# S5 chunk matrices built on the chip instead of read back from DRAM, in a hybrid S5 and MoE layer

## The chip, the cores and the metric

One core of a Trainium2 chip runs one layer of a decoder in f32. The metric is the device time of one execution in microseconds (us). The engines are PE (TensorE, products and transposes), ACT (ScalarE), DVE (VectorE), POOL (GpSimd) and SP (SyncE, which only issues DMAs here).

## The reference

For 256 tokens of width 1024, a token mixer (S5, a diagonal complex state space model with 48 groups of 16 channels and 64 states) runs beside a four-head attention into 256 fixed memory rows. Both read one input projection, and their outputs are concatenated, projected and normed. A mixture of 32 experts, four for each token, follows, and a second norm. Cut to what matters here:

```
xin = x @ w_in                                  # 768 channels u for S5, 256 for the queries
bu  = einsum('gph,blgh->lbgp', B, u)            # complex
x_l = A * x_(l-1) + bu_l                        # scan over the tokens, by group and state
y   = re(einsum('ghp,lbgp->blgh', C, x)) + d_skip * u
y   = gelu(y);  y = y * sigmoid(y @ w_glu + b_glu)
h   = layer_norm(alpha * x + concat(y, xattn(queries, mem)) @ w_out)
out = layer_norm(alpha * h + moe(h))            # 32 experts, top 4, w_gu and w_down in f32
```

## The kernel before, in words

The scan is cut into 32 chunks of 8 steps. A chunk's outputs are the sum of two products: its own inputs by a matrix made of K[k] = C A**k B (k from 0 to 7, with the skip added at k = 0), and the state ahead of the chunk by C A**k. For each group the first matrix is block Toeplitz: for output step t and input row k (k = 7 - s for input step s) it is K[t + k - 7], and zero where that is negative.

K is made at L544 to L566. Products `kb` of `ca_pad` with the powers `m1p` go through `kr` (ACT copies) and transposes `kc` into `k_sb`, where POOL adds the skip `dsk`. Then it goes through DRAM: L584 writes zeros in front of K in `kd`, three stores at L589 write K behind them, and three loads at L596 read overlapping rows of 2048 words, so that the eight partition blocks of a tile `tj` hold K shifted by one step each. The products at L745 (`yb<-tj,u_sb`, 96 by count) use it; behind them on PE come the memory's share of the output projection (`yp<-wo,att`), the second group of `yb` products (`yb<-m,xs`), the gate (`zp`), the rest of the output projection, the router, and the experts.

Around this place, in program order: `m1_turned` (transposes and ACT copies), the power tables `m20` (DVE, with a sum on POOL), the memory's keys (`kps`), the chunk states (`sip`, `stp`), the scores of the attention (`sc`), `m21` and `m22`, the softmax (`mx` on DVE, `prob` on ACT), the scan of the states on DVE (`tw`, `gt`, then `xs`), the memory's values (`vmp`), `pTp` (transposes of `prob`) and `pv`. PE, ACT and DVE keep the program's order (`pin`). DMAs are issued on SP. A DMA takes one of eight semaphores in turn, so a ninth waits for the first to land.

Large tiles share a pool of 22 buffers of 128 x 2048 words (`NBIG`, `big_tile`). A load into one of them is issued when the buffer's last reader is done. The experts' weights, 12 tiles an expert (8 `gu` at L1081, 4 `dn` at L1088), go through the same pool, so their loads start when the tiles of the stages ahead are given up, and then follow PE's release of the experts' tiles before.

Of the kernel before, what the change touches and what calls it, by code (L numbers as in the profile page):

```python
# [9 lines left out]
F32 = mybir.dt.float32  # L10
# [6 lines left out]
P = 128  # L17
D = 1024          # model width
NT = 256          # tokens
KT = D // P       # k-tiles of the model width  # L20
MIX = 768         # S5 channels
NG, NS, NH = 48, 64, 16   # S5 groups, states of a group, channels of a group
Q, NC = 8, 32     # steps of a chunk, chunks (t = Q * c + s)
NE = 32           # experts
CAP = 64          # slots of an expert in one round
ALPHA = 2.0 ** 0.25
LN_EPS = 1e-5
MISS = 8192.0     # put between the ranks of an expert's tokens and of all others
# [8 lines left out]
RND = 12582912.0  # 1.5 * 2**23: adding it rounds to the nearest integer  # L37
# [3 lines left out]
def kernel(  # L41
# [55 lines left out]
    def pin(ins):  # L97
        """Keeps an engine's instructions in the order of this program."""
        key = (ins.ins.engine, id(nc.cur_bb.bb))
        if key in last_of:  # L100
            tc.add_manual_dep(
                ins.ins, last_of[key],
                mybir.DependencyInfo(mybir.DependencyClass.NoSync, mybir.DependencyReason.DATA), reason="order",
            )
        last_of[key] = ins.ins.name
        return ins

    class Ordered:
        """An engine whose instructions keep the order of this program."""
# [26 lines left out]
    # ------------------------------------------------------------------ constants; a warm tensor engine  # L136
# [5 lines left out]
    def busy(n):  # L142
        """Products nobody needs, that keep the tensor engine's clock up."""
        ps = bank("busy") if n else None
        for _ in range(n):
            mm(ps[:, 0:P], ones, ones, True, True)

    busy(9)
    sga, sgc = small("sga", (P, 1)), small("sgc", (P, 1))   # by the half of the partitions: - + and + -
# [4 lines left out]
    # ------------------------------------------------------------------ loads, in the order of need  # L154
# [23 lines left out]
    dsk = small("dsk", (NH, NG, NH))  # L178
    SP.dma_start(dsk.rearrange("p g h -> p (g h)"), d_skip.partition_broadcast(NH))
# [11 lines left out]

    tt(dsk, dsk, ident[0:NH, 0:NH].unsqueeze(1).to_broadcast([NH, NG, NH]), ALU.mult, G)   # D[g, h] (h' = h)

    # ------------------------------------------------------------------ S5: the parameters, [(twice, p), group]
# [8 lines left out]
    # B: ba = [re; im], bb = [im; re]; C: ca = [re; - im], cb = [im; - re]; all [(re | im, p), g, h]  # L203
# [19 lines left out]
    # ------------------------------------------------------------------ x transposed  # L223
# [20 lines left out]
    # ------------------------------------------------------------------ projections  # L244
    # u, channels on partitions, in order of (s, c) for t = 8 c + s; from there to u_sb[(k, h), g, c], k = 7 - s
# [38 lines left out]
    def dve_exp(o, in_, n):  # L284
        """o = exp(in_), by 2**k * e**r; in steps."""
# [15 lines left out]
    def together(*chains):  # L301
        """The steps of independent chains, in turns."""
        chains = list(chains)
        while chains:
            chains = [c for c in chains if next(c, chains) is not chains]
# [11 lines left out]
    # sin and cos of ang = k pi + r, |r| <= pi / 2  # L317
# [3 lines left out]
    def series(o, coef, last):  # L321
        """o = last * sum of coef[k] r2**k"""
# [5 lines left out]
    def angle():  # L328
# [15 lines left out]
        # (sgn has come in between)  # L344
# [4 lines left out]
    def sign():  # L349
        """(-1)**k"""  # L350
# [14 lines left out]
    # powers of A = mag (cs + i sn): apw[:, 0 | 1, k] = re | im of A**k  # L365
# [14 lines left out]
    # coef = (A - 1) / lam  # L380
# [15 lines left out]
    # tables [re; re] and [- im; im]  # L396
# [31 lines left out]
    # ------------------------------------------------------------------ S5: A**k B and C A**k, [(re | im, p), gl, k, h]  # L428
    ptmp = [big_tile(f"ptmp{k}") for k in range(2)]

    def power(name, j, k0, m):
        """A**k m for k0 <= k < k0 + 8 and the groups from 16 j on."""
# [27 lines left out]
    # ------------------------------------------------------------------ S5: W[c] = (cs + i sn)**(8 c), [(a, p), (j, l), c]  # L460
# [43 lines left out]
    # the damping of a chunk, zero where a new sequence starts  # L504
# [4 lines left out]
    # queries of the memory, transposed: [(2 heads, 64), pair, n]  # L509
# [27 lines left out]
    # ------------------------------------------------------------------ memory: keys, scores  # L537
# [4 lines left out]
    # response of a chunk's outputs to its own inputs, [(k, h'), g, h], with the skip at k = 0; in memory behind zeros,  # L542
    # from where a chunk's matrix is T[(k, h'), t, g, h] = K[t + k - 7]
    kt_ = big_tile("k_sb")  # L544
    k_sb, zt = kt_[:, 0:768].rearrange("p (g h) -> p g h", h=NH), kt_[0:48, 768:1024]
    G.memset(zt, 0.0)
    kr = big_tile("kr")[:, 0:1536].rearrange("p (b n) -> p b n", b=3)
    for b in range(3):
# [8 lines left out]
        S.copy(kr[:, b, :], ps)  # L557
    for b in range(3):
        ps = bank(f"kc{b}")
        for l in range(4):  # L560
            tr(ps[:, P * l : P * l + P], kr[:, b, P * l : P * l + P])
        S.copy(
            k_sb.rearrange("p (j l) h -> p l j h", j=4)[:, 4 * b : 4 * b + 4],
            ps.rearrange("p (l j h) -> p l j h", l=4, j=4)[:, :, :, 0:NH],
        )
    tt(k_sb[0:NH], k_sb[0:NH], dsk, ALU.add, G)  # L566
    dbg("@M1B", None)
    # A**k B transposed, in its place: [(k, h), gl, (re | im, p)]
# [12 lines left out]
    dbg("@KW", None)  # L581
    row = 15 * 256
    kd = dram.tile([48, row], F32, tag="kd", name="kd")
    SP.dma_start(kd[:, 0 : 7 * 256].rearrange("r (k n) -> r k n", k=7), zt.unsqueeze(1).to_broadcast([48, 7, 256]))  # L584
    dbg("@KD", None)
    tj = []
    for j in range(3):
        kj = kd[16 * j : 16 * j + 16, :]
        SP.dma_start(  # L589
            bass.AP(tensor=kj.tensor, offset=kj.offset + 7 * 256, ap=[[256, Q], [row, NH], [1, 256]]),  # L590
            k_sb[:, 16 * j : 16 * j + 16, :].rearrange("p g h -> p (g h)"),
        )
    for j in range(3):
        t = big_tile(f"tj{j}")
        kj = kd[16 * j : 16 * j + 16, :]
        SP.dma_start(t, bass.AP(tensor=kj.tensor, offset=kj.offset, ap=[[256, Q], [row, NH], [1, 2048]]))  # L596
        t = t.rearrange("p (t g h) -> p t g h", t=Q, g=16)
        tj += [t[:, :, g, :] for g in range(16)]

# [11 lines left out]
    # ------------------------------------------------------------------ S5: what each chunk adds to its end's state  # L611
# [14 lines left out]
    # re, im of [(a, p), (j, l), c], g = 12 j + 2 l + a  # L626
# [14 lines left out]
    for i in range(2):  # L641
# [8 lines left out]
        scores.append(sc)  # L650

# [29 lines left out]
    # ------------------------------------------------------------------ S5: states between chunks  # L681
# [6 lines left out]
    # conj(W) S, then the damped sum over the chunks before  # L688
# [34 lines left out]
    # states before each chunk: W times that, one chunk later; [(re | im, p), (r, a), c]  # L723
# [15 lines left out]
    # ------------------------------------------------------------------ S5: outputs, [(j, c), t, gl, h]; bank l % 3  # L739
# [5 lines left out]
    for gl in range(12):  # L745
        for j in range(4):
            mm(
                y_out(gl, j).rearrange("p (t h) -> p t h", h=NH), u_sb[:, 12 * j + gl, :], tj[12 * j + gl],
                gl % 4 == 0, False, True,
            )  # L750
# [34 lines left out]
    # channels on partitions: tiles 0-3 are channels 192 j + (0 .. 127), tiles 4, 5 pairs of the rest  # L785
# [24 lines left out]
    # the router's weights behind the norm's: (n g + b) W + rb = n (g W) + (b W + rb)  # L810
# [29 lines left out]
    # ------------------------------------------------------------------ output projection, first norm  # L840
# [9 lines left out]
    def norm_of_stats(n):  # L850
        """The mean and 1 / sqrt(var + eps), after norm_stats of both halves."""
# [8 lines left out]
    iota64 = keep_t("iota64", (P, CAP))                                # slot - MISS  # L860
# [5 lines left out]
    lower = keep_t("lower", (P, P))                                    # 1 where the row comes before the column  # L866
# [36 lines left out]
    # ------------------------------------------------------------------ router  # L903
# [35 lines left out]
    def chosen(i, lgp):  # L939
        """The mask of each token's four experts."""  # L940
# [10 lines left out]
    def ranks(i, ps):  # L951
        """Ranks among an expert's tokens, MISS below."""
        stt(rk[:, i, :], msk[:, i, :], -MISS, ps, ALU.mult, ALU.add)

    def up_bias(n, sel):
        """Both halves of the first product, [(half of the columns, slot), 512] each: the bias first."""
# [26 lines left out]
    # ------------------------------------------------------------------ experts  # L983
    def gather(n, rank, base, between=lambda: None):
        """The tokens of an expert's slots, transposed; rank is [P, 1] by token tile."""
# [19 lines left out]
    def gates_t(n, og, k):  # L1005
        """The gates of one or two experts' slots, slots on partitions."""
# [324 lines left out]
```

## Time and profile before

| what | value |
|---|---|
| median of 3 runs | 1120.77 us (1116.89 to 1122.39) |
| the profiled execution (its span) | 1121.0 us |
| PE busy | 1053.1 us (94%) |
| DVE, ACT, POOL busy | 286.4, 142.5, 53.9 us |
| DMA | 428.56 MB, mean 382 GB/s |
| chain that ended last | PE 55%, DMA 42% of the span |
| of it, DMA tj<-kd | 4% |

The busy time of PE counts products in flight, so 94% does not say that PE is the limit. The chain follows the last instruction back to what released it at each step; a DMA in it is a time in which an engine had nothing else to do but wait for that transfer.

### The profile page before, as it was taken

To read this page: it belongs to the slowest core of one execution; us is meant where nothing else is said; L and a number is where in the kernel's file an instruction comes from. 1 tells how busy PE (TensorE), PEld (TensorE's weight loads), DVE (VectorE), ACT (ScalarE), POOL (GpSimd) and SP (SyncE) were. 2 spreads that over 40 slices of the span, in tenths; PEclk is the share of its full clock that TensorE was granted. 3 is DMA by queue.
4 is the path that set the end of the run, shared out by engine and by line. 5 is a ranking of instruction groups with operands and counts; after the bars stand their busy time and mean duration, and the time that the engine had idled before them with its cause. 6 is when DMAs were issued, how large, how long until landed. Compare 5 with 4: busy or idle time off the path is not lost.

```text
span 1121.0 us, 13652 instructions
## 1 busy us (share of the span) xinstructions
PE 1053.1 (94%) x5721; PEld 486.0 (43%) x5721; DVE 286.4 (26%) x631; ACT 142.5 (13%) x270; POOL 53.9 (5%) x53
## 2 busy tenths in 40 slices
PE   9975999999999999999999898999899999999994
PEld 8863754444444444444434343423343343434331
DVE  7984142121212111212111212111121212121204
ACT  4441201000000101010100000000000000010002
POOL 1650030000000000000000000000000000000001
PEclk9986999999999999999999999999999999999998
DMA  8988989999999999999999999999999999999992
GB/s 236 230 172 166 378 356 392 415 415 416 415 415 417 415 417 416 417 416 416 416 416 415 417 415 416 417 416 416 402 416 417 416 416 416 415 416 416 415 404 78
DMA packets 90022, 428.56 MB, mean 382 GB/s; under 512 B 15918, under 2 KB 19474, under 8 KB 56804
## 3 DMA queue, kind: packets, MB, share of 16 engines
q1 hardware_dynamic: 89668, 427.11, 98.1%
q8 instruction: 47, 0.77, 0.3%
q10 hardware_dynamic: 288, 0.52, 0.1%
q14 instruction: 19, 0.16, 0.0%
HBM read 425.03 MB, written 2.57 MB: 381 GB/s over the span
## 4 chain that ended last, share of the span: by engine, by line
PE 55%; DMA 42%; DVE 1%; SPq 1%; issue 0%; ACT 0%; ACTq 0%; POOL 0%; DVEq 0%
PE gu_e L122 22%; DMA gu_e<-in_exp_w_gu_dram 22%; DMA dn_e<-in_exp_w_down_dram 15%; PE dn_e L122 13%; PE xgp_e L122 7%; PE cb_e L122 4%; DMA tj<-kd 4%; PE yp L122 2%; DMA win<-in_l_w_in_dram 1%; PE zp L122 1%; PE atp_e L125 1%; PE yb L122 1%; DMA mem_sb<-in_mem_dram 1%; PE qps L122 1%; PE kps L122 1%; SPq L168 0%
## 5 line engine op out<-in xcount | busy, mean ns | idle before, releaser
L122 PE MATMUL gu_e<-gu_e,xg_e 128*64 128x512 f32 x2048 | 457.2, 595 | 27.9 <-DMA gu_e<-in_exp_w_gu_dram 27.3
L122 PEld LDWEIGHTS gu_e<-gu_e,xg_e 128*64 128x64 f32 x2048 | 141.3, 137 | 337.6 <-issue 250.2
L122 PE MATMUL dn_e<-dn_e,xl_te 128*64 128x512 f32 x1024 | 226.8, 596 | 0.7 <-ACT xl_te L116 0.7
L122 PEld LDWEIGHTS dn_e<-dn_e,xl_te 128*64 128x64 f32 x1024 | 70.7, 137 | 154.0 <-issue 126.5
L1028 DVE TENSOR_SCALAR xl_e<-gu_e 128x512 f32<-128x512 f32 x32 | 22.1, 692 | 430.6 <-PE gu_e L122 430.6
L122 PEld LDWEIGHTS xgp_e<-oh_e,h_sb 128*128 128x128 f32 x1024 | 118.1, 192 | 7.3 <-issue 4.3
L122 PE MATMUL xgp_e<-oh_e,h_sb 128*128 128x64 f32 x1024 | 118.2, 274 | 0.0
L1056 DVE COPY y_e<-dn_e 64x512 f32<-64x512 f32 x32 | 21.9, 683 | 252.7 <-PE dn_e L122 252.7
L116 ACT ACTIVATE sg_e<-xl_e 128x512 f32<-128x512 f32 x32 | 20.2, 630 | 404.3 <-DVE xl_e L1028 404.3
L122 PE MATMUL cb_e<-y_e,ogT_e 128*128 128x512 f32 x120 | 55.8, 604 | 0.0
L116 ACT COPY y_e<-dn_e 64x512 f32<-64x512 f32 x32 | 18.6, 581 | 257.6 <-DVE y_e L1056 250.4
L116 ACT COPY xg_e<-xgp_e 128x512 f32<-128x512 f32 x32 | 18.7, 585 | 155.3 <-PE xgp_e L122 155.3
L128 DVE TENSOR_TENSOR acc<-acc,cb_e 128x512 f32<-128x512 f32 x56 | 36.2, 683 | 6.6 <-PE cb_e L122 6.6
L122 PEld LDWEIGHTS cb_e<-y_e,ogT_e 128*128 128x128 f32 x120 | 21.7, 190 | 32.5 <-issue 29.7
L122 PE MATMUL gu_e<-bgu,ident 32*64 32x512 f32 x256 | 34.8, 612 | 0.0
L131 DVE TENSOR_SCALAR oh_e<-iota,rk 128x64 f32<-128x64 f32 x62 | 13.0, 252 | 66.7 <-PE xgp_e L122 66.7
L1125 POOL MEMSET bd<- 128x1280 f32 x1 | 1.2, 1164 | 583.4 <-PE gu_e L122 583.4
L1030 DVE TENSOR_SCALAR xr_e<-gu_e 128x512 f32<-128x512 f32 x32 | 22.1, 692 | 3.1 <-PE gu_e L122 0.2
L1031 DVE SCALAR_TENSOR_TENSOR xr_e<-xr_e,xl_e 128x512 f32<-128x512 f32 x32 | 22.0, 689 | 0.5
L1032 DVE TENSOR_TENSOR xr_e<-xr_e,sg_e 128x512 f32<-128x512 f32 x32 | 22.0, 687 | 0.6 <-DVE og_e L131 0.2
L122 PE MATMUL ups<-xT,win 128*128 128x256 f32 x96 | 21.5, 382 | 0.4 <-DMA win<-in_l_w_in_dram 0.4
L122 PE MATMUL yp<-wo,ymT 128*128 128x512 f32 x48 | 20.9, 595 | 0.0
(283 smaller groups left out, 580.4 us busy)
## 6 DMA issues: line engine op xcount, KB each, us to landing
gu_e<-in_exp_w_gu_dram SPq DMA_DIRECT2D x256, 1024.0 KB, 19.9
dn_e<-in_exp_w_down_dram SPq DMA_DIRECT2D x127, 1024.0 KB, 20.1
win<-in_l_w_in_dram SPq DMA_DIRECT2D x8, 512.0 KB, 10.2
wo<-in_w_out_dram SPq DMA_DIRECT2D x3, 1024.0 KB, 41.8
tj<-kd SPq DMA_DIRECT2D x3, 1024.0 KB
wgl<-in_l_s_w_glu_dram SPq DMA_DIRECT2D x2, 768.0 KB, 9.9
x_sb<-in_x_dram SPq DMA_DIRECT2D x2, 512.0 KB, 3.6
mem_sb<-in_mem_dram SPq DMA_DIRECT2D x1, 1024.0 KB
```

What stands on the lines that cost most here:

```text
L116: return f if name == "dma_start" else lambda *a, **k: pin(f(*a, **k))
L122: pin(PE.matmul(o, lhsT, rhs, start=start, stop=stop, skip_group_check=shared))
L125: pin(PE.transpose(o, in_, ident if idn is None else idn))
L128: return (eng or V).tensor_tensor(out=o, in0=x0, in1=x1, op=op)
L131: return (eng or V).tensor_scalar(out=o, in0=x0, scalar1=s1, scalar2=s2, op0=op0, op1=op1)
L1028: V.tensor_scalar(out=xl_, in0=ps[0], scalar1=7.0, scalar2=None, op0=ALU.min)
L1030: V.tensor_scalar(out=xr, in0=ps[1], scalar1=7.0, scalar2=-7.0, op0=ALU.min, op1=ALU.max)
L1031: V.scalar_tensor_tensor(out=xr, in0=xr, scalar=1.0, in1=xl_, op0=ALU.add, op1=ALU.mult)
L1032: V.tensor_tensor(out=xr, in0=xr, in1=sg, op=ALU.mult)
L1056: eng(y[:, 512 * dh : 512 * dh + 512], ps[dh][64 * dh : 64 * dh + 64, :])
L1125: G.memset(t[:, 0:width], 0.0)
```

## The change

K no longer goes through DRAM. `k_sb`, `kd` and the seven DMAs around it are gone. `kr` has 144 columns a group, 16 of zeros in front of 128, and the skip is added there, on all partitions. Three tiles `tz` are allocated and filled with zeros by POOL at the place where `k_sb` was. Behind the scores, each of the three gets two sets of four transposes out of `kr` (the second set from 16 columns earlier, which shifts by one step), each evicted by ACT into one step t of `tz`; then five ACT copies move pairs of steps to other partition blocks, 32 partitions further for two steps. `yb` reads its matrices from `tz`. For the skip on all partitions `d_skip` is loaded by four DMAs instead of one, and a DVE reduction makes the mask `same`. (Comments are taken out as well; those lines are not shown.)

```diff
-    dsk = small("dsk", (NH, NG, NH))
-    SP.dma_start(dsk.rearrange("p g h -> p (g h)"), d_skip.partition_broadcast(NH))
+    dsk = small("dsk", (P, 12, NH))
+    for j in range(4):
+        SP.dma_start(
+            dsk[32 * j : 32 * j + 32].rearrange("p g h -> p (g h)"),
+            d_skip[192 * j : 192 * j + 192].partition_broadcast(32),
+        )
...
-    tt(dsk, dsk, ident[0:NH, 0:NH].unsqueeze(1).to_broadcast([NH, NG, NH]), ALU.mult, G)
+    same = small("same", (P, NH))
+    V.tensor_reduce(
+        out=same, in_=ident.rearrange("p (j r) -> p r j", j=4)[:, 0:NH, :], axis=AX.X, op=ALU.add
+    )
+    tt(dsk, dsk, same.unsqueeze(1).to_broadcast([P, 12, NH]), ALU.mult, G)
...
-    kt_ = big_tile("k_sb")
-    k_sb, zt = kt_[:, 0:768].rearrange("p (g h) -> p g h", h=NH), kt_[0:48, 768:1024]
-    G.memset(zt, 0.0)
-    kr = big_tile("kr")[:, 0:1536].rearrange("p (b n) -> p b n", b=3)
+    kr_t = big_tile("kr")
+    kr = kr_t[:, 0 : 12 * 144].rearrange("p (b n) -> p b n", b=12)
+    G.memset(kr[:, :, 0:NH], 0.0)
+    tz = []
+    for b in range(3):
+        tz.append(big_tile(f"tz{b}"))
+        G.memset(tz[b], 0.0)
...
-        S.copy(kr[:, b, :], ps)
-    for b in range(3):
-        ps = bank(f"kc{b}")
-        for l in range(4):
-            tr(ps[:, P * l : P * l + P], kr[:, b, P * l : P * l + P])
-        S.copy(
-            k_sb.rearrange("p (j l) h -> p l j h", j=4)[:, 4 * b : 4 * b + 4],
-            ps.rearrange("p (l j h) -> p l j h", l=4, j=4)[:, :, :, 0:NH],
-        )
-    tt(k_sb[0:NH], k_sb[0:NH], dsk, ALU.add, G)
+        S.copy(kr[:, 4 * b : 4 * b + 4, NH:144], ps.rearrange("p (l n) -> p l n", l=4))
+    tt(kr[:, :, NH : 2 * NH], kr[:, :, NH : 2 * NH], dsk, ALU.add, G)
...
-    dbg("@KW", None)
-    row = 15 * 256
-    kd = dram.tile([48, row], F32, tag="kd", name="kd")
-    SP.dma_start(kd[:, 0 : 7 * 256].rearrange("r (k n) -> r k n", k=7), zt.unsqueeze(1).to_broadcast([48, 7, 256]))
-    dbg("@KD", None)
-    tj = []
-    for j in range(3):
-        kj = kd[16 * j : 16 * j + 16, :]
-        SP.dma_start(
-            bass.AP(tensor=kj.tensor, offset=kj.offset + 7 * 256, ap=[[256, Q], [row, NH], [1, 256]]),
-            k_sb[:, 16 * j : 16 * j + 16, :].rearrange("p g h -> p (g h)"),
-        )
-    for j in range(3):
-        t = big_tile(f"tj{j}")
-        kj = kd[16 * j : 16 * j + 16, :]
-        SP.dma_start(t, bass.AP(tensor=kj.tensor, offset=kj.offset, ap=[[256, Q], [row, NH], [1, 2048]]))
-        t = t.rearrange("p (t g h) -> p t g h", t=Q, g=16)
-        tj += [t[:, :, g, :] for g in range(16)]
...
+    tv = [t.rearrange("p (g t h) -> p g t h", t=Q, h=NH) for t in tz]
+    for b in range(3):
+        for a in range(2):
+            ps = bank(f"kc{b}{a}")
+            for l in range(4):
+                tr(ps[:, P * l : P * l + P], kr[:, 4 * b + l, NH - NH * a : NH - NH * a + P])
+            S.copy(tv[b][:, :, Q - 1 - a, :], ps.rearrange("p (g h) -> p g h", h=2 * NH)[:, :, 0:NH])
+        for m, rows in ((1, ((32, 64), (64, 96), (96, 128))), (2, ((64, 128),)), (3, ((96, 128),))):
+            for r0, r1 in rows:
+                S.copy(
+                    tv[b][r0:r1, :, Q - 2 - 2 * m : Q - 2 * m, :],
+                    tv[b][r0 - 32 * m : r1 - 32 * m, :, Q - 2 : Q, :],
+                )
+    tj = [tz[(g % 12) // 4][:, P * (4 * (g % 4) + g // 12) :][:, 0:P] for g in range(NG)]
```

## Rows read from the trace of the kernel before

**Rows 1.** The page, rate of DMA in 40 slices of 28 us.
```profile
GB/s 236 230 172 166 378 356 392 415 415 416 415 415 417 415 417 416 417 416 416 416 416 415 417 415 416 417 416 416 402 416 417 416 416 416 415 416 416 415 404 78
```
**Rows 2.** A window: us, busy by engine, PEclk, DMA share, GB/s.
```profile
190.00:560.00 370.00, 370.00 (x1942) 157.39 (x1943) 70.23 (x146) 33.96 (x62) 0.00 (x0) 1.00 1.02 416
```
**Rows 3.** Waits of the load queue, 172 to 200 us: total, times, longest.
```profile
SPq L1088 <- PE gu_e L122: 9.6, 3, 7.1
```
**Rows 4.** The chain in order of time: start us, us, what.
```profile
62.63 39.72 DMA tj<-kd
...
121.61 15.89 PE zp L122 x96
...
172.51 13.96 PE gu_e L122 x64
```
**Rows 5.** Timeline of PE: start us, us, what, [idle before <- releaser].
```profile
49.61 1.53 PE L125 MATMUL kc<-ident,kr 128*128 128x128 f32 x12
...
64.34 2.00 PE L122 MATMUL sc<-att 64*128 64x256 f32 x16
...
80.61 4.22 PE L125 MATMUL pTp<-ident,prob 128*128 128x128 f32 x16 [7.17 <-ACT prob L116]
...
88.03 0.41 PE L122 MATMUL yb<-tj,u_sb 128*32 128x128 f32 x4
...
102.39 5.27 PE L122 MATMUL yb<-tj,u_sb 128*32 128x128 f32 x90 [11.48 <-DMA tj<-kd]
107.59 7.13 PE L122 MATMUL yp<-wo,att 128*128 128x512 f32 x16
114.66 2.83 PE L122 MATMUL yb<-m,xs 128*32 128x128 f32 x96
```
**Rows 6.** Windows of PE's work and pauses, columns as in rows 2.
```profile
76.00:87.00 11.00, 5.85 (x24) 4.17 (x26) 8.32 (x13) 9.40 (x30) 0.27 (x2) 0.53 1.05 152
87.00:90.00 3.00, 1.44 (x14) 0.56 (x10) 2.93 (x3) 1.83 (x2) 0.00 (x0) 1.00 0.87 98
90.00:107.00 17.00, 5.20 (x90) 4.41 (x91) 6.89 (x8) 0.04 (x1) 0.00 (x0) 0.51 0.77 152
```
**Rows 7.** Timeline of DVE, from several windows.
```profile
44.36 0.27 DVE L116 TENSOR_TENSOR s<-cv 128x24 f32<-128x24 f32 x2
...
55.10 2.15 DVE L116 TENSOR_TENSOR mv__473<-mv__473 128x24 f32<-128x24 f32 x3
...
72.64 3.66 DVE L116 TENSOR_SCALAR mx<-mx 128x4 f32<-128x4 f32 x1
...
95.22 1.89 DVE L116 TENSOR_TENSOR xs<-tw 64x744 f32<-64x744 f32 x2
```
**Rows 8.** Groups by form, ACT, to 165 us: busy us, mean ns | idle before.
```profile
L116 ACT COPY ut<-ups 128x512 f32<-128x512 f32 x3 | 2.9, 1112 | 2.9 <-PE ups L122 2.9
...
L116 ACT COPY kr<-kb 128x512 f32<-128x512 f32 x3 | 1.8, 587 | 1.2 <-PE kb L122 1.2
...
L116 ACT COPY k_sb<-kc 128x256 f32<-128x256 f32 x3 | 1.1, 372 | 0.1
```
**Rows 9.** Timeline of ACT: the first exponential of the softmax.
```profile
76.41 0.47 ACT L116 ACTIVATE prob<-sc,mx 128x256 f32<-128x256 f32 x1 [11.32 <-DVE mx L116]
```
**Rows 10.** Timeline of SP: start us, us of issuing, what.
```profile
26.80 0.47 SPq L413 DMA_DIRECT2D mem_sb<-in_mem_dram  x1
...
108.42 15.09 SPq L1081 DMA_DIRECT2D gu_e<-in_exp_w_gu_dram  x8
```
**Rows 11.** Groups by form, POOL: busy us, mean ns | idle before.
```profile
L1125 POOL MEMSET bd<- 128x1280 f32 x1 | 1.2, 1164 | 583.4 <-PE gu_e L122 583.4
```
**Rows 12.** Timeline of POOL: start us, us, what, [idle before <- releaser].
```profile
44.31 0.30 POOL L546 MEMSET k_sb<- 48x256 f32 x1
...
51.69 5.29 POOL L128 TENSOR_TENSOR k_sb<-k_sb,dsk 16x768 f32<-16x768 f32 x1 [7.08 <-DVE s L116]
...
67.14 9.01 POOL L128 TENSOR_TENSOR m<-m,ptmp 128x2048 f32<-128x2048 f32 x2 [0.35 <-POOL r L607]
```

More of the change, by code (lines that the diff above doesn't have):

```diff
@@ L747 @@
             mm(
-                y_out(gl, j).rearrange("p (t h) -> p t h", h=NH), u_sb[:, 12 * j + gl, :], tj[12 * j + gl],
+                y_out(gl, j).rearrange("p (t h) -> p t h", h=NH), u_sb[:, 12 * j + gl, :], tj[12 * j + gl].rearrange("p (t h) -> p t h", h=NH),
                 gl % 4 == 0, False, True,
```

## The prediction

> **What bounds the kernel now.** I read the page's rates by slice first, then the chain of waits, then windows around the two places that they point to, and last the timelines of the engines there. [rows 1] shows three parts: a start in which DMA moves 166 to 236 GB/s, a ramp of three slices at 356 to 392, and a long flat stretch near 416 GB/s. [rows 2] says what the flat stretch is: from 190 to 560 us the queues move 416 GB/s with no gap. It is the load of the experts' weights, and nothing in the change touches its rate. So the end can move only if this stretch begins earlier. What begins it stands in [rows 3]: between 172 and 200 us the load queue's issues wait for PE, for gu_e products that give a buffer back, so at that point all 22 big buffers are full and the transfers have caught up with PE. From there the rest of the kernel hangs on the time at which PE reaches the first expert's products, 172.51 us [rows 4]. A microsecond by which PE gets there earlier should be a microsecond off the end, one for one, as long as the loads can again fill the buffers by then.
>
> What holds PE up before that is one item: the chain waits 39.72 us, up to 102.39, for tj to land [rows 4], the loads that the change removes. Not all of the 39.72 us is lost. In [rows 5] PE has other work until 88.03; there the first yb products (a chunk's response to its own inputs) start, and after six of them PE sits idle for tj, 11.48 us on end. Behind the wait the granted clock is half (0.51 in [rows 6]), so that 90 products take 5.27 us where the 96 of the later yb group take 2.83 [rows 5]. From 76 to 107 us the queues move 98 to 152 GB/s [rows 6].
>
> **Removed.** The four stores to kd, the three loads tj, and the wait for them. If yb runs from 88.03 without a pause, at the full clock (1.00 from 87 to 90 us in [rows 6]), its 96 products take 2.83 us and end at 90.9. The yp products behind it need wo and att, which PE did not wait for before, and take 107.59 to 114.66 = 7.1 us. The second yb group (states, with xs) then starts at 97.9 instead of 114.66: **16.7 us earlier**. Its other input, xs, is ready at 95.22 + 1.89 = 97.1 [rows 7], so DVE is the next to be late, but by less. If the clock came back late, yb at half takes 5.27 x 96 / 90 = 5.6, 2.8 us more, and yp for as long again 1.4 more; 4.2 us is my bound. [rows 5, 6] have it at full again 5 to 6 us after PE takes up work (80.61 to 87, 102.39 to 107). I take the full clock, because pTp and pv fill the 7 us ahead of yb, as they do now.
>
> **Added to ACT, the price that counts.** 21 instructions go in front of the softmax: six evictions of 128x256, and fifteen copies of 512 elements a partition (32 or 64 partitions). An eviction of this size takes 372 ns, a 512-element copy 587 [rows 8]; the partitions do not enter. Sum 6 x 0.372 + 15 x 0.587 = 11.0 us. In the profile ACT idles 11.32 us just there, up to 76.41, where the softmax starts after mx [rows 9]. So the gap nearly holds the block. It can start when sc is done, 66.34, plus four transposes at the 1.53 / 12 = 0.13 us of kc's [rows 5], 0.5, less 0.1 for what moves ahead of it (below): 66.7. It ends at 77.8. The softmax starts **1.4 us later** than now, and pTp, pv, yb and xs with it (xs at 98.5). Bounds of a shifted copy: not under the 0.372 us of half its elements (then the block ends at 74.5, mx decides, and the softmax starts 1.2 us earlier than now), and up to 1.112 us, the price of ut [rows 8], whose writes are scattered word by word; then the block takes 18.9 us, and the softmax starts 9.2 us later. The copies here write runs of 32 words, nearer to kr's evictions than to ut's, so I take 0.587.
>
> **Moved and added on PE.** Twelve kc transposes leave the path at 50 us, 1.5 us [rows 5], and 24 come after sc, 3.1 us. These, and vmp behind them, which may also wait a few us for a PSUM bank that ACT gives back, lie in the idle stretch of 7.17 us before pTp [rows 5]; without that cover they would cost those 3.1 us.
>
> **Added at the start.** d_skip comes in four DMAs instead of one: three more issues on SP in front of mem_sb, whose own takes 0.47 us, at 26.80 [rows 10]. Memory keys and K then come up to 1.4 us later, against the 1.5 us that PE saves: net 0.1 earlier. One small reduction on DVE lies in the time before the first load lands. On SP nothing else moves; seven issues disappear, and the loads of wo, wgl and x that sat among them can only come earlier.
>
> **POOL.** Three fills of 128x2048 and a small one. At 1.16 us for 1280 columns [rows 11] a fill of 2048 is 1.8, so 5.4 us together. They would stand where the small k_sb fill stands now, 44.31, and be done near 50, before kr is there. The skip's addition shrinks from 16x768, 5.29 us, to 128x192, about 0.4 by m's 2048 in 4.5 [rows 12]. That matters to DVE: when the present addition got to run, DVE's three tiny mv_ products took 2.15 us in place of some 0.5 [rows 7]. So DVE gets about 1.2 us back, and with it POOL's m sums, which end at 67.14 + 9.01 = 76.15 [rows 12] and release mx (the 3.66 us row of [rows 7] ends just behind them). mx moves to 75.2 and stays in front of ACT's 77.8. For the fills the bounds are 0 and, if each held DVE as the additions do, 5.4 + 0.4 in place of 1.6: 4.2 us on DVE, the softmax at 80.6, 2.8 us behind my 77.8. I take 0: the k_sb fill ran from 44.31 to 44.61, and DVE's two s products of two SBUF inputs took 0.27 together beside it [rows 7, 12].
> [...]
>
> **Big buffers.** tz takes three of the 22 from about 44 us on, where tj took its three at 61, and kr stays until 67; k_sb's is gone. If that leaves one short, it is a load of wgl or wo that waits, and zp, the first to need wgl, starts at 121.61 now [rows 4] and about 106 then. The last of them can be issued when prob has been read, by 80.61 + 4.22 + 1.4 = 86.2 [rows 5], and has 20 us to spare, with no tj in its way.
>
> **Sum.** PE reaches the second yb group 16.7 - 1.4 = 15.3 us earlier, at 99.4, and from there on the work is what it was, so the first expert starts at 157.2. Do the weights follow? Their first tiles take buffers that come free at yb's end (about 92) and with xs (98.5); 20 tiles of 2.5 us (1.05 MB at 416 GB/s) are there near 149, before 157. So the shift reaches the end: 1121.0 - 15.3 = 1105.7. The profiled span is 0.2 us above the median of the runs, 1120.77; I say **1105.5 us**. The three runs lie 0.5% apart (1116.89 to 1122.39), so 0.5% is also about what this kernel's measurement tells from no change.
>
> **Rivals.**
> *The front eats half of it* (0.15). Fills that hold DVE (+2.8), a clock that comes back late (+4.2), or shifted copies at ut's price (9.2 in place of 1.4, +7.8): one alone gives 1108 to 1113, two together up to 1117.5. For it: the softmax has no slack, by [rows 7, 9] it starts with mx. Against: the rows by which each was taken at its low end.
> *The end does not move by PE's shift* (0.06). If the weights could not begin before 108.42, as now [rows 10], because wo, wgl and x stay slow without tj (152 GB/s in [rows 6]), 20 tiles would end at 158.4, and only what the queues lose later could be won: in the three slices of the ramp (378, 356, 392 against 416, 28 us each) some 8 us. With a delay of the front on top the time is 1113 to 1119. Against: in the first of these slices the queues, rid of tj, move 378 GB/s at once [rows 1].
> *Slower* (0.04): the shifted copies wait on one another, each for the writes of the one before, and ACT's block becomes the path. It breaks even where it lasts 11.0 + 15.3 = 26.3 us, at (26.3 - 2.2) / 15 = 1.61 us a copy; at 2.2, twice ut, it lasts 35.2, the softmax starts at 101.9 instead of 76.41, and the time is 1120.8 - 16.7 + 25.5 = 1129.6. Against: the rows nearest to these copies are all under 1.12 us.
> *yb still waits* (0.02), now for a tz that is late, because a fill stands behind a buffer still in use: between 1106 and 1121, by the hold.
>
> **Numbers.** The forecast has 0.73; its own range is 1100 (the softmax 1.2 us earlier instead of 1.4 later, 1102.9, less half the runs' spread) to 1109. With the front's rival the range is 1100 to 1114. Faster by over 0.5% (under 1115.2): 0.73 + 0.13 + 0.03 + 0.01 = 0.90. Within 0.5%: 0.06, the rest of the three mild rivals. Slower: 0.04.
>
> **What would show it.** In the profile after: yb in one piece of about 2.8 us near 89.4, with no DMA in front; the second yb group near 99.4; ACT busy without a gap from 66.7 to 77.8 with copies of 0.5 to 0.6 us, and softmax after it; POOL fills at 44 to 50 with DVE's tiny products beside them at their usual price; the first gu_e near 157; the flat 416 GB/s from about 175. I am wrong if the copies take over 1 us, if the fills stretch DVE's chain past 60 us, or if the weights' queue no longer waits on PE at the first expert, for then the end was not PE's to move.

## The result, and the profile after

The changed kernel takes 1108.56 us (median of 4 runs, 1108.34 to 1110.52) against 1120.9 of the kernel before on the same chip: ratio 0.9894, 95% interval 0.9876 to 0.9911, so 1.1% faster and clear of noise. The forecast was 1105.5, its range 1100 to 1114. The profiled execution has a span of 1108.8 us, 12.2 less than before; it is the longest of the four (1110.52 us), so its rows are those of one execution.

The rates of DMA by slice, as in [rows 1]:

```profile
GB/s 230 240 139 274 408 258 408 417 415 416 414 416 416 416 415 416 417 416 417 416 417 415 415 416 416 416 416 415 400 417 416 416 416 416 415 417 416 415 406 82
```

The flat stretch is what it was. The ramp is another: 408 GB/s from the fifth slice on (about 111 us), and then a dip to 258 that [rows 1] doesn't have. In the dip, from 139 to 149 us (107 GB/s), the queues have caught up with PE and wait for buffers.

PE's timeline, to be laid beside [rows 5]:

```profile
65.66 2.00 PE L122 MATMUL sc<-att 64*128 64x256 f32 x16
...
84.14 4.08 PE L125 MATMUL pTp<-ident,prob 128*128 128x128 f32 x16 [2.19 <-ACT prob L116]
88.91 3.68 PE L122 MATMUL pv<-pT,att 128*64 128x256 f32 x16 [0.69 <-ACT pT L116]
92.52 3.42 PE L122 MATMUL yb<-tz,u_sb 128*32 128x128 f32 x96
95.87 7.13 PE L122 MATMUL yp<-wo,att 128*128 128x512 f32 x16
102.94 2.83 PE L122 MATMUL yb<-m,xs 128*32 128x128 f32 x96
...
160.78 2.79 PE L122 MATMUL gu_e<-gu_e,xg_e 128*64 128x512 f32 x12 [0.68 <-ACT xg_e L116]
```

The first yb products run in one piece, with no DMA in front. The second group starts at 102.94 instead of 114.66, the first expert at 160.78 instead of 172.51: both 11.7 us earlier. The load queue still waits for PE at the first experts, as in [rows 3] (waits of SP, 160 to 190 us):

```profile
SPq L1088 <- PE gu_e L122: 10.8, 4, 7.1
```

ACT's block, in ACT's timeline, begins at 68.32 and ends where the softmax starts, 79.93, which was 76.41 in [rows 9]:

```profile
68.32 0.77 ACT L116 COPY tz<-kc 128x256 f32<-128x256 f32 x2 [1.92 <-issue]
69.12 3.13 ACT L116 COPY tz<-tz 32x512 f32<-32x512 f32 x5
...
79.93 0.47 ACT L116 ACTIVATE prob<-sc,mx 128x256 f32<-128x256 f32 x1
```

POOL's timeline (first fence) has the fills where they were expected, and DVE's (second fence) its tiny products beside them and the maximum of the softmax:

```profile
44.82 5.31 POOL L557 MEMSET tz<- 128x2048 f32 x3
53.07 2.92 POOL L128 TENSOR_TENSOR kr<-kr,dsk 128x192 f32<-128x192 f32 x1 [2.94 <-ACT kr L116]
```

```profile
45.05 0.49 DVE L116 TENSOR_TENSOR s<-e__485 128x24 f32<-128x24 f32 x4
...
55.41 1.05 DVE L116 TENSOR_TENSOR mv__478<-mv__478 128x24 f32<-128x24 f32 x3
56.38 2.28 DVE L116 TENSOR_TENSOR m<-cab,tab 128x2048 f32<-128x2048 f32 x1
...
71.27 3.56 DVE L116 TENSOR_SCALAR mx<-mx 128x4 f32<-128x4 f32 x1
```

Windows (columns as in [rows 2]) show the granted clock below full speed (means of 0.66, 0.57 and 0.51) in three short stretches. In the first of them PE had waited 2.28 us for mem_sb:

```profile
35.00:40.00 5.00, 4.46 (x21) 4.33 (x22) 5.00 (x4) 2.35 (x4) 5.00 (x4) 0.66 1.08 350
...
73.00:77.00 4.00, 4.00 (x14) 3.26 (x12) 3.19 (x4) 3.90 (x8) 1.81 (x1) 0.57 0.81 144
...
87.00:94.00 7.00, 6.31 (x53) 3.91 (x57) 6.86 (x7) 3.69 (x8) 0.00 (x0) 0.51 0.67 190
```

### The profile page after: what moved, and what is told of

The parts are those of the page before. It is cut to its first block, busy times and chain, and to the rows that moved or that the text cites. A ratio compares the mean times of both kernels' runs of the same rounds, so it can differ in the third digit from the quotient of the medians.

```text
span 1108.8 us, 13702 instructions
## 1 busy us (share of the span) xinstructions
PE 1056.9 (95%) x5733; PEld 487.9 (44%) x5733; DVE 285.5 (26%) x632; ACT 153.0 (14%) x288; POOL 55.6 (5%) x56
## 4 chain that ended last, share of the span: by engine, by line
PE 58%; DMA 37%; ACT 2%; DVE 1%; SPq 1%; issue 1%; ACTq 0%; POOL 0%; DVEq 0%
PE gu_e L122 24%; DMA gu_e<-in_exp_w_gu_dram 22%; PE dn_e L122 13%; DMA dn_e<-in_exp_w_down_dram 13%; PE xgp_e L122 7%; PE cb_e L122 4%; PE yp L122 3%; DMA win<-in_l_w_in_dram 1%; PE zp L122 1%; ACT tz L116 1%; PE atp_e L125 1%; DMA mem_sb<-in_mem_dram 1%; PE qps L122 1%; PE kps L122 1%; ACT prob L116 1%
```

## The experiments

Twelve kernels ran, each timed in five rounds against the kernel before. In those marked *, yb reads zeros, so each chunk's response to its own inputs is left out. "Left" is what the queues still had to move after 190 us, summed over the packets that end later; the rate beside it is that of a window. Times are in us.

| kernel | second yb | first expert | GB/s, 149 to 190 | left, MB | span | median | ratio |
|---|---|---|---|---|---|---|---|
| before | 114.66 | 172.51 | 359 | 377.19 | 1121.0 | 1120.9 | |
| after | 102.94 | 160.78 | 383 | 372.32 | 1108.8 | 1108.56 | 0.9894 |
| 1 round trip beside it, into DRAM | 101.71 | 159.55 | 386 | 371.68 | 1106.6 | 1108.35 | 0.9883 |
| 2 copies twice | 108.68 | 166.53 | 348 | 374.78 | 1114.4 | 1117.25 | 0.9962 |
| 3 skip's loads late | 98.56 | 156.41 | 381 | 370.50 | 1104.3 | 1106.68 | 0.9869 |
| 4 copies shared with DVE | 97.53 | 155.77 | 382 | 370.18 | 1103.1 | 1104.80 | 0.9847 |
| 5 both | 97.22 | 155.72 | 383 | 370.15 | 1103.9 | 1105.56 | 0.9859 |
| 6 before, yb without tj* | 107.59 | 165.38 | 415 | 374.64 | 1114.9 | 1116.09 | 0.9953 |
| 7 before, tj in 16-row loads | 99.58 | 157.43 | 406 | 370.96 | 1105.2 | 1107.05 | 0.9872 |
| 8 before, tj alone | 105.63 | 163.49 | 416 | 374.36 | 1114.4 | 1116.45 | 0.9947 |
| 9 before, yb without tj, tj held* | 97.44 | 159.24 | 417 | 374.18 | 1116.5 | 1119.78 | 0.9979 |
| 10 as 9, plain rows of weights* | 97.56 | 155.45 | 391 | 369.77 | 1102.3 | 1105.36 | 0.9858 |
| 11 as 9, the pattern on weights* | 97.27 | 159.12 | 417 | 374.35 | 1116.6 | 1116.64 | 0.9946 |
| 12 as 11, no overlap* | 97.21 | 155.11 | 417 | 372.53 | 1111.6 | 1114.17 | 0.9927 |

Two columns are to be read together. In every row the span is 190 us, plus what is left at 416 GB/s, plus 23 to 27 us. So the end goes with how much the queues have moved by then. The rate says what held them: at 348 to 391 GB/s they had gaps, waiting for PE to give buffers back; at 415 to 417 they had none, and were simply late (run 7 lies between). The expectations name their theories A and B anew in each run.

### 1. The round trip's traffic, put back beside the change

```diff
+    SP.dma_start(kd[:, 0 : 7 * 256]..., tz[0][0:48, 0:256]...)
+    for j in range(3):
+        SP.dma_start(<kd behind the zeros>, tz[j][:, 0:256])
+    for j in range(3):
+        td = dram.tile([P, 2048], F32, tag=f"td{j}", name=f"td{j}")
+        SP.dma_start(td, <the overlapping rows of kd>)
```

> The changed kernel with the transfers of the old round trip put back, with nothing waiting for them: the zero store, three stores to kd (of zeros), and three loads of 2048-word overlapping rows, which go to DRAM instead of SBUF, so another 3 MB is written. The results do not use them. Theory A (the end follows PE's arrival at the experts, and PE lost its wait for tj): no wait, no loss; 1108.6 us, at most 2 more from loads that come later. Theory B (the gain is the 3.8 MB and the slow queues that went): the gain is given back, 1118 to 1121.

1108.35 us (0.9868 to 0.9897): as fast as without the traffic. That spoke for PE's arrival alone, but too soon. These loads end in DRAM, and their 8 KB packets took 311 to 355 ns, where those of tj into SBUF took 737 to 957 (means over 5 us each) between 65 and 100 us in the kernel before. The bytes were put back, the slow transfer was not. Runs 9 to 12 make good for that.

### 2. Each shifted copy twice

```diff
-            for r0, r1 in rows:
+            for r0, r1 in rows + rows:
```

> The changed kernel with each of the fifteen shifted copies on ACT made twice, so ACT's block in front of the softmax is 15 x 0.626 = 9.4 us longer. A: every us of it goes to the end, 1118 us; second yb group 9.4 later than in the changed kernel. B: the end stays at 1108.6, give or take 1, for no transfer has changed.

1117.25 us (0.9950 to 0.9974). The softmax starts at 87.97, the second yb group 5.74 us later than in the changed kernel, and the span is 5.6 longer. By the medians the difference is 8.7 us, near the 9.4 of A. B is out: with free queues (348 GB/s, gaps) a delay of PE reaches the end, in the profiles one for one.

### 3. The skip's four loads later in the program

```diff
-    for j in range(4): SP.dma_start(dsk[...], d_skip[...])      # ahead of mem_sb
...
     SP.dma_start(wv, mem_w_v...)
+    for j in range(4): SP.dma_start(dsk[...], d_skip[...])
```

> The changed kernel with the four loads of d_skip issued behind wv instead of ahead of mem_sb, and POOL's product with the mask moved to its use. A, with the clock's drop at 35.8 us caused by the later mem_sb: mem_sb is issued near 26.2, the clock stays at full, PE has its 2.6 us back and the scores end near 65, ACT's block 2.6 earlier: 1106.0. If the delay of PE's front has another cause than these loads: 1108.6.

1106.68 us (0.9855 to 0.9884). sc starts at 63.56 instead of 65.66, the softmax at 77.84, and the granted clock from 35 to 40 us is 1.00 instead of 0.66. pv takes 2.00 us and yb 2.83, both at full clock. In the profiles the second yb group is 4.4 us earlier and the span 4.5 shorter.

The time is near A's 1106.0, but not for A's reason. On SP the four loads still went out ahead of the memory's, although they stand behind them in the program:

```profile
25.38 1.81 SPq L421 DMA_DIRECT2D dsk<-in_l_s_d_dram  x4
...
27.70 0.47 SPq L415 DMA_DIRECT2D mem_sb<-in_mem_dram  x1
```

mem_sb is issued at 27.70, as in the changed kernel (27.74), and not near 26.2. The earlier front did not come back in run 5, which has the same edit. By the medians the gain is 1.9 us, and the intervals of the two ratios overlap (0.9855 to 0.9884, 0.9876 to 0.9911). So no run shows a gain by this edit.

### 4. Ten of the fifteen copies on DVE

```diff
+        if b == 0:
+            shifts(b, S.copy)
...
         sums.append(sm)                  # behind the second mx
+    shifts(1, V.tensor_copy)
...
             S.mul(prob...)               # behind the reciprocals
+    shifts(2, V.tensor_copy)
```

> The changed kernel with ten of the fifteen shifted copies moved from ACT to DVE, five behind mx and five behind the reciprocals of the softmax, where DVE idles. A: the softmax starts with mx at 74.9 instead of 79.9, and the end comes 5 us earlier, 1103.6, less what xs gains of delay on DVE (its slack to PE is 2.3 us). B: 1108.6.

1104.80 us (0.9834 to 0.9860), clear of the changed kernel's interval and the lowest median of all, though not clear of runs 5 and 10. ACT's and PE's timelines show the next limits, mx and then xs:

```profile
75.09 0.47 ACT L116 ACTIVATE prob<-sc,mx 128x256 f32<-128x256 f32 x1 [1.10 <-DVE mx L116]
```

```profile
98.15 2.61 PE L122 MATMUL yb<-m,xs 128*32 128x128 f32 x88 [0.20 <-DVE xs L116]
```

### 5. Runs 3 and 4 together

> The changed kernel with both edits of before: ten shifted copies on DVE, and d_skip loaded behind wv. With the ten copies away the softmax waits for mx (POOL's m sums, done near 74.9), not for ACT's block; an earlier PE front then has no one to give its time to. A: the same as with the split alone, 1104.8, at most 1 less. If the two gains simply added up: 1104.8 - 1.9 = 1102.9.

1105.56 us (0.9844 to 0.9874): no more than run 4, as A said. The second yb group waits for xs, 1.13 and 0.44 us:

```profile
97.22 0.43 PE L122 MATMUL yb<-m,xs 128*32 128x128 f32 x8 [1.13 <-DVE xs L116]
```

So an earlier PE would have had nothing to gain here. It was not earlier, though: sc starts at 65.82, and mem_sb is issued at 28.37. Whether the gains of 3 and 4 are the same microseconds is therefore not shown.

### 6. The kernel before, with yb reading zeros

```diff
-                ..., u_sb[:, 12 * j + gl, :], tj[12 * j + gl],
+                ..., u_sb[:, 12 * j + gl, :], zer.rearrange("p (t h) -> p t h", h=NH),
```

> The kernel before with its whole round trip through DRAM, loads of tj into SBUF included, but the first yb products read a tile of zeros instead of tj: the chunks' own response and the skip are left out of the output, and nothing waits for tj. A: yb near 88, the second yb group near 98, zp perhaps held some 2 us for wgl, which lands near 107 while tj's transfers are under way: 1104 to 1108. B (the transfers themselves cost the time): 1119 to 1121.

1116.09 us (0.9939 to 0.9966), between the theories. ACT's timeline says why the front gained little: the tiles of tj that nobody read were given to the softmax as its output, which then waited for them.

```profile
86.12 0.47 ACT L116 ACTIVATE prob<-sc,mx 128x256 f32<-128x256 f32 x1 [21.20 <-DMA tj<-kd]
```

The wait had moved, so this run settles nothing by itself; run 9 is its repair.

### 7. tj in loads of 16 rows

```diff
-        SP.dma_start(t, <8 blocks of 16 rows of kd>)
+        for k in range(Q):
+            SP.dma_start(t[16 * k : 16 * k + 16], <16 rows of kd from block k>)
```

> The kernel before, round trip kept and used, with each of the three tj loads (outermost 8 blocks of 16 rows) cut into eight loads of 16 rows of 2048 words, the same bytes from the same places. If the slowness of these loads (3 MB in 40 us, packets of 8 KB at 0.72 to 0.96 us) comes from how one load of that shape is spread, they land before 88 and the wait is gone without any work for ACT: 1104 to 1107. If it comes from reading the same rows many times: no change, 1121, or slower by the 24 issues on SP at about 0.5 us each.

1107.05 us (0.9856 to 0.9888): the round trip is still there, and the kernel is as fast as the changed one. yb starts at 89.76 without a wait. A window while the loads run:

```profile
65.00:82.00 17.00, 9.92 (x56) 8.11 (x54) 14.52 (x11) 5.25 (x21) 13.00 (x5) 0.89 1.02 137
```

All 16 DMA engines are taken (share 1.02), yet they move only 137 GB/s. Two things had changed at once: the cut, and that tj was alone, since wo waited until 82.68 behind the 24 loads on SP.

### 8. tj alone, uncut

```diff
-    wo += load_wo(0)
+    wo0 = big_tile("wo0")...
...
             S.mul(prob...)
+    S.copy(wo0[0:1, 0, 0:1], prob[0:1, 1, 3, 0:1])
+    SP.dma_start(wo0, ov[0:P, 0:2, :])
```

> The kernel before with its round trip whole and its three loads of tj uncut; only the first load of wo behind them is held until the softmax has ended on ACT (one element of its tile is written by ACT there, so some 83 us instead of 63), and with it what stands behind it on SP. Theory A (tj came late because wo, wgl and x were on the queues with it; alone, 3 MB at the 134 GB/s of the run with cut loads take 23 to 25 us from 62.6): tj lands at 86 to 89, the first yb products follow pv without a wait, the second yb group starts near 98 to 102, time 1105 to 1110 us. Theory B (it was the cut into loads of 16 rows that made the transfer faster): tj lands after 98, and with the loads of wo later still the time is 1116 to 1124 us. If B holds and A falls, the reason given for the run with cut loads is wrong again.

1116.45 us (0.9933 to 0.9961): neither theory. A window of the transfer alone, and PE's wait behind it:

```profile
64.00:83.00 19.00, 11.49 (x58) 9.21 (x58) 16.45 (x15) 7.34 (x26) 12.19 (x5) 0.86 0.51 116
```

```profile
93.55 5.09 PE L122 MATMUL yb<-tj,u_sb 128*32 128x128 f32 x90 [5.65 <-DMA tj<-kd]
```

With the queues to itself tj moves at 116 GB/s with the DMA engines half taken (share 0.51), and lands at 93.5 instead of 102.4. So of the gain of run 7 in landing (102.4 to about 88.5), some 9 us are from the order and 5 from the cut, although run 7 issued its first load 2 us later (63.03 instead of 60.98).

### 9. Run 6 with tj's buffers held

```diff
+    for b in range(3):                   # behind the yb products
+        G.tensor_copy(zer[:, 4 * b : 4 * b + 4], tj[16 * b][:, 0, 0:4])
```

> The kernel before with yb reading a tile of zeros instead of tj, so each chunk's response to its own inputs is left out; stores and loads of the round trip stay, and POOL reads a few columns of each tj behind the yb products, so that no other tile takes tj's buffers early. Theory A (the wait for tj is what the change took out, and nothing else holds the second yb group): the softmax starts at 76 as before, yb follows pv near 88, the second yb group starts at 97 to 100, the first expert at 155 to 158, time 1103 to 1108 us; that is 0 to 5 us below the changed kernel, since the block of ACT copies isn't there. Theory B (the end hangs on the loads behind tj, of wgl and of the experts' first weights, which still come as late as before): first expert at 170 to 173, time 1117 to 1121 us.

1119.78 us (0.9968 to 0.9989). PE does what theory A said, and the time what theory B said. The second yb group starts at 97.44, 17.2 us earlier than before, and the time is 0.2% less. PE's timeline and a window:

```profile
108.30 15.89 PE L122 MATMUL zp<-yT,wgl 128*128 128x256 f32 x88 [1.98 <-DMA wgl<-in_l_s_w_glu_dram]
```

```profile
149.00:190.00 41.00, 40.33 (x246) 21.28 (x244) 12.58 (x41) 7.25 (x14) 1.93 (x2) 1.00 1.02 417
```

zp waits for wgl, which stood beside tj on the queues, and the experts' first load is issued at 108.24, as before (108.42). The queues then run without a gap and are late all the same.

### 10 and 11. The same bytes, as plain rows and in the pattern

```diff
-        SP.dma_start(t, <the overlapping rows of kd>)
+        SP.dma_start(t, w_gu[0, NE - 1][P * j : P * j + P, :])                    # 10
+        SP.dma_start(t, bass.AP(..., ap=[[256, Q], [row, NH], [1, 2048]]))        # 11, on the same weights
```

> As the kernel that held tj for POOL and let yb read zeros (each chunk's response to its own inputs is left out), with one edit: the three loads of 128 rows of 8 KB that nobody on PE waits for read contiguous rows of an expert's weights instead of the overlapping rows of kd. The same bytes go into the same tiles at the same place of the queue; the stores to kd stay. Theory A (the end hangs on both: PE's arrival and the queues; the slow load held the queues, so wo, wgl and the experts' first tiles came late although PE was early): rows of weights take some 315 ns a packet, 3 MB land by 70 to 72, wo and wgl follow in under 15 us, zp waits for nothing, the first expert is at 156 to 158, 870 to 873 us of queue time (at 416 GB/s) are left at 190 us... that is 369.5 to 371 MB left there, and the time is 1102 to 1108 us. Theory B (what stays of the round trip, its stores and its 3 MB of loads, costs the same at any rate, or zp's wait for wgl had another cause): 373 MB or more left at 190, time 1114 to 1120 us.

> As the run before it, but the three loads read the weights with the overlapping pattern that the kernel before uses on kd (8 blocks 1 KB apart, in each 16 rows 15 KB apart, 8 KB each). Each chunk's response to its own inputs is left out here too. Theory A (the pattern makes it slow, 8 outer steps or the overlap, whatever tensor it reads): 8 KB packets of 560 to 960 ns as on kd, the loads land at 95 to 102, zp waits for wgl, time 1115 to 1120 us. Theory B (reading a tensor that was just written makes it slow): packets of some 315 ns, landing by 72, time 1102 to 1108 us.

(The 870 to 873 us in the first text is a slip; 369.5 to 371 MB at 416 GB/s are 888 to 892.)

Run 10 takes 1105.36 us (0.9844 to 0.9872), run 11 takes 1116.64 (0.9932 to 0.9959): A in both. Between 9 and 10 differ only three transfers that PE never waits for: their rate, and their issue, which is 3.9 us earlier since it doesn't wait for the stores to kd. Together that is worth 14 us; run 12 below, issued as early as run 10, leaves about 9 for the rate alone. A window of run 10 while they run, and PE behind it:

```profile
60.00:68.00 8.00, 7.86 (x118) 6.56 (x107) 8.00 (x5) 3.52 (x7) 5.00 (x3) 1.00 1.01 414
```

```profile
104.44 15.96 PE L122 MATMUL zp<-yT,wgl 128*128 128x256 f32 x96
```

The DMA issues from 55 to 120 us (KB each, median us to landing), first of run 10, then of run 11, say how wo fares behind them:

```profile
wo<-in_w_out_dram SPq DMA_DIRECT2D x2, 1024.0 KB, 9.5
```

```profile
wo<-in_w_out_dram SPq DMA_DIRECT2D x2, 1024.0 KB, 42.3
```

And since run 11 reads weights, it is not the tensor just written that makes tj slow; it is the pattern. (The median of run 11 is 3 us below that of run 9; in the profiles, 1116.6 and 1116.5 us long, nothing shows why.)

### 12. Eight outer steps without overlap

```diff
-            ap=[[256, Q], [row, NH], [1, 2048]]
+            ap=[[2048, Q], [2048 * Q, NH], [1, 2048]]
```

> As the run that reads the weights with the overlapping pattern (yb reads zeros, so each chunk's response to its own inputs is left out), but without the overlap: the pattern has the same 8 outer steps of 16 rows of 8 KB, and its 128 rows are the 128 different rows of a weight tile, 64 KB apart within a block. Theory A (8 outer steps leave half of the queues' engines without work, or the order in which the rows land is bad, whatever is read): slow as with the overlap, landing at 95 to 102, some 374 MB left at 190 us, time 1115 to 1120 us. Theory B (it is the rows that overlap, each byte read eight times from 240 KB): packets of 315 to 350 ns, landing by 75, 369.5 to 371 MB left at 190 us, time 1102 to 1108 us. In between (packets of some 315 ns, but half the rate, 200 GB/s, landing near 78) would mean 8 engines at full speed and still 1102 to 1108 us.

1114.17 us (0.9911 to 0.9943), nearer to A. SP issues tj's loads in runs 10, 11 and 12 as follows:

```profile
55.61 3.78 SPq L598 DMA_DIRECT2D tj<-in_exp_w_gu_dram  x3
```

```profile
59.70 2.06 SPq L599 DMA_DIRECT2D tj<-in_exp_w_gu_dram  x3
```

```profile
55.74 3.79 SPq L599 DMA_DIRECT2D tj<-in_exp_w_gu_dram  x3
```

In run 12 that is 4.0 us earlier than in run 11, and they land at 95.6 instead of 99.7, so they take as long. The overlap costs nothing that shows; the eight outer steps are enough. The last 2 MB of difference to run 11 are about those 4 us. Against run 10, which issues them at the same time, the pattern costs 8.8 us by the medians and 9.3 by the spans.

## Why the prediction was right, and where it missed

**What bounds the kernel: right for this change, but said too simply.** The forecast had the end follow PE one for one, because the load queue waits for PE at the first expert. Between before and after it does (11.7 us at the first expert, 12.2 at the end), and again in run 2. But run 9 shows that PE's wait was only one of two things behind tj. With PE's wait gone and the slow transfer kept, the time falls by 0.2%; the loads of wo, wgl and the experts, held up by it, then set the end, although PE is early. The change gains 12 us because it takes both away at once. The second rival ("the end does not move by PE's shift") described this mechanism: weights that can't begin before 108.42, and a time of 1113 to 1119. It is real, and runs 9 and 11 are it (first load of the experts at 108.24 and 108.12, medians of 1119.78 and 1116.64). It didn't decide here for the reason that the forecast gave against it: without tj the queues are fast at once. The first experts' load is issued at 98.73 instead of 108.42, wo lands in 5.7 us instead of 41.8, and the loads have caught up with PE by 139 us.

**yb's wait (16.7 us): right.** It is gone.

**ACT's block (11.0 us): right, mis-sized by 0.6.** It takes 11.6. A shifted copy costs 0.626 in place of 0.587, 15 times; the evictions 0.374, as taken. Between copies of 32 and of 64 partitions the profile shows no difference (616 and 617 ns). The copies don't wait on one another (five in 3.13 us), so the slower rival's 1.61 us is far away.

**The start (net 0.1 earlier): wrong by 1.4 us in the profile.** sc starts at 65.66 instead of 64.34. The three more issues on SP move mem_sb's from 26.80 to 27.74, 0.9 us, as bounded. But PE waits longer for it, and behind that wait the granted clock is at half for a while (0.50 over 36 to 39 us, 0.66 over 35 to 40), so that memT (transposes of the memory's rows) takes 3.45 us instead of 1.94. The rows of before and after:

```profile
34.62 1.94 PE L125 MATMUL memT<-ident,mem_sb 128*128 128x128 f32 x16 [1.66 <-DMA mem_sb<-in_mem_dram]
```

```profile
35.54 3.45 PE L125 MATMUL memT<-ident,mem_sb 128*128 128x128 f32 x16 [2.28 <-DMA mem_sb<-in_mem_dram]
```

Over 35 to 40 us the clock is 0.66 to 0.68 in the profiles of after and of runs 4 and 5, and 1.00 in runs 1 to 3, so the clock's part of it is not fixed by the change. Nor is the rest: the kernels with the front of before (before and runs 6 to 12) have sc between 63.57 and 65.82, those with the changed one (after, 1, 2 and 4) between 64.05 and 65.88. How much of the 1.4 us is the change's own is not shown.

**The clock at yb (full): half wrong.** The forecast took the full clock and had up to 4.2 us as a bound. pv runs at half and yb in part: pv takes 3.68 us, against 2.72 in the trace of before, and yb 3.42 instead of 2.83, together 1.6. The reason given, that pTp and pv fill the time ahead of yb, is not enough: here they did, with PE's waits of 2.19 and 0.69 us in front of them, and the clock fell to half (0.51 over 87 to 94 us); in run 3 they did too, behind waits of 1.75 and 1.23, and it stayed full.

These three add up: 1.4 late at sc, 0.2 for the first transposes and the issue behind them, 0.6 for the block, and 1.4 net between softmax and second yb. That is the 3.5 us between 99.4 and 102.94, and so most of the 3 us by which the time was missed. The likeliest rival, a front that eats more, has part of the truth, by the clock that came back late, but neither by its fills nor by copies at ut's price.

**POOL (fills at 0): right.** Three fills take 5.31 us, 1.77 each against the 1.8 of the estimate, and DVE's products of two SBUF inputs beside them cost 0.12 each (four in 0.49), as in the trace of before at 45.38, where POOL ran nothing (four in 0.49). The skip's addition is another matter: it was taken at 0.4 us and took 2.92, and DVE's mv_ products beside it 1.05 in place of 2.15 [rows 7]. DVE came out 1.15 us ahead all the same (m at 56.38, 57.53 in the trace of before), against 1.2 expected; mx at 74.8, against 75.2. So three of DVE's tiny products took 2.15 and 1.05 us beside POOL's additions, while beside its fills they kept the 0.12 each.

**Big buffers: right.** The loads of wo and wgl, and the fills, waited for no tz, and zp not for wgl. Behind them the loads of gb and of the first expert wait 6.0 and 1.9 us for yb, which reads tz among others.

## What to carry to other kernels

A slow transfer in front of a stage that is bound by loads can cost twice, as here: PE waited for it (11.48 us on end), and the loads behind it on the queues were late (the experts' first at 108.42, and at 98.73 without it). A late PE alone (run 2, its span 5.6 us above the changed kernel's) and late loads alone (run 9, 0.2% under the kernel before) each held the end, so look at how much the queues have moved by a fixed time, not only at the chain of waits. Before replacing a round trip through DRAM, look at the rate of its loads: this one, cut into loads of 16 rows and let onto the queues by itself, left the kernel as fast as the change that removes it (run 7). And where copies take the transfer's place, share them among engines until the next input (here mx, then xs) decides.

## What the hardware showed that was not expected

**tj's load is slow by its pattern.** 128 rows of 8 KB move at 116 GB/s alone, with the DMA engines half taken (share 0.51, run 8); contiguous rows into the same tiles move at 414, with all of them taken (share 1.01, run 10). The share is not the whole of it: half of 414 would still be some 207, and in run 1 the same reads into DRAM moved 197 GB/s between 65 and 80 us, with some eight 8 KB packets in flight at a time. Into SBUF it is 116, and 16-row loads, with all 16 engines taken (share 1.02), give only 137 (run 7). So there the packets themselves were slow: one takes some 580 ns between 65 and 83 us in run 8, against 315 in run 10.
The reads alone don't make them slow, since into DRAM they took 311 to 355 ns a packet (run 1), and neither does the overlap (39.9 us from the first issue to the last landing in run 12, 40.0 in run 11). What it is in the pattern that slows a packet on its way into SBUF is not shown: no run here changed only the order in which the rows land.

**A lower clock behind a short wait.** Ahead of memT PE waits for mem_sb. In the profiles of after and of runs 4 and 5 that wait is 2.28, 2.37 and 2.68 us, the granted clock over 35 to 40 us is 0.66 to 0.68 (in after 0.50 over 36 to 39), and memT takes 3.45, 2.65 and 3.48 us. In before and in runs 1, 2, 3, 7 and 8 the wait is 0 to 1.66 us, the clock is 1.00, and memT takes 1.94. The wait alone doesn't settle it: in run 3 the clock is 0.71 over 73 to 77 us (vmp takes 8.86 us, 7.07 in run 1), behind waits of 1.49, 0.71 and 0.17 us, and 1.00 over 87 to 94 (pv 2.00, yb 2.83), behind waits of 1.75 and 1.23. What decides there, and why mem_sb lands later in some of these kernels than in others, stays open.
